# Shared-key attention scores: stacked hi/lo products against whole fp32 products on alternating row halves

## The chip, the core and the metric

The program runs on one core of a Trainium2 chip. The metric is the device time of one execution in microseconds. The kernel before took 2250.57 us, the median of 3 runs (2250.23 to 2251.85).

## The reference

Four transformer layers in fp32 over 256 tokens and a model width of 1024: two layers of a first block, then two of a second. What matters here is attention in which four query heads of 64 dimensions share one key head:

```python
# first block, per layer: 8 query heads, 2 key heads, window of 128, sinks
q = apply_rope(rms_norm(to_heads(sw_q, SWA_HEADS), q_norm_g[l]), cos, sin)
k = apply_rope(rms_norm(to_heads(sw_k, SWA_KV_HEADS), k_norm_g[l]), cos, sin)
scores = jnp.einsum('bnqkgd,bnskd->bnkgqs', qb, k_band).astype(jnp.float32) * scale
...
# second block (NSA), per layer: 8 query heads, 2 key groups, three branches
s = jnp.einsum('btghd,bngd->bghtn', qi, k_cmp).astype(jnp.float32) * scale   # compressed
s = jnp.einsum('btghd,bgtnd->bghtn', qi, k_sel).astype(jnp.float32) * scale  # selected
s = jnp.einsum('btghd,bsgd->bghts', qi, k_win).astype(jnp.float32) * scale   # window
return g_blk[..., 0:1] * o_cmp + g_blk[..., 1:2] * o_slc + g_blk[..., 2:3] * o_win
```

With 256 tokens, the selected and the window branch each come to causal attention over all keys, and the compressed branch has 15 keys, held as 16. The first block also has stick-breaking attention with 8 heads that each own their keys; the second has a gated MLP, a short convolution, latent attention (MLA, 8 heads with their own keys), and cross attention.

## The kernel before, in words

The core has three SBUF pools by size and eight PSUM banks. A bank (128 partitions x 512 fp32) is taken by `b.ps()`, in rotation. `mm` (L413) issues every matmul and `tr` (L419) every transpose. Large products are split: a value is rounded to fp32r (hi) by ACT (`split`, L570), and DVE subtracts it to get the rest (lo, L571); products of hi and lo parts are one pass each. A product of plain fp32 operands runs as two passes on TensorE, so one `mm` shows as two MATMULs in the trace.

`attend` runs four-head groups in rounds. Round r does the weights of group r-1 (scale the probabilities, L1610; transpose them; split them), the values of group r-2, the scores of group r, the preparation of group r+1, and then fills the gap with pieces of other matrix products (`gap`). The order of instructions on each engine is the order of this code. A layer of the first block has 2 groups of class `SharedHeads`, in rounds with 2 of `StickBreaking`; a layer of the second block has 4 `SharedHeads` groups and 2 of `OwnHeads` (MLA), in the order nsa, mla, nsa, nsa, mla, nsa. That is 12 `SharedHeads` groups in all. The generator `compressed` runs beside the second block's rounds.

The scores of a `SharedHeads` group, for 4 heads and two halves m of the queries:

- `stack_queries` has ACT round the transposed queries (L845) onto one half of the 128 rows and DVE put the rest (L846) on the other half, for each key head. `stack_keys` copies the first 128 keys onto both halves in fp32 (L855), the rounded keys onto both halves (L856, L857), and the rest of the keys on one half (L858).
- `SharedHeads.scores` then does, for m = 0, four fp32 products of 128 rows and 128 columns in one bank; for m = 1, in two more banks and per head, one fp32r product of 128 rows and 256 columns, and one of 64 rows with the rest of the keys.
- `softmax` reads the three banks with eight DVE operations, one for each m and head (`masked`, L816), and ACT exponentiates each.

`StickBreaking.scores` is written in another way: each of its heads lies on rows 0 to 63 or 64 to 127 by its parity, the products are plain fp32 of 64 rows, consecutive ones alternate between the two row halves, and they go to four banks. Per group these are four products of 256 columns and four of 128.

`SharedHeads.values` multiplies the weights with v: a product of 128 output rows for the hi part of the weights, and one of 64 for the lo part. `own_values`, for groups whose heads own their keys, has heads with even number use 64 output rows and odd ones 128; its last product is plain fp32.

Of the kernel before, what the change touches and what calls it, by code (L numbers as in the profile page):

```python
# [17 lines left out]
ALU = mybir.AluOpType  # L18
# [244 lines left out]
class Build:  # L263
# [546 lines left out]
    def masked(self, ps, mask, n, w, factor, first, nm):  # L810


        p = self.t("b2", [P, n, w])
        t = self.masks["window" if mask == "window" else "causal"][:, 2 * P - w:]
        for i in range(n):
            self.nc.vector.tensor_tensor_reduce(p[:, i], ps[:, i * w:i * w + w], t, factor(i), first(i), ALU.add, ALU.min,  # L816
                                                nm[:, i:i + 1])
        return p
# [18 lines left out]

    def stack_queries(self, dst, ps, m):


        nc = self.nc
        for g in range(2):
            r, o = slice(64 * g, 64 * g + 64), slice(64 - 64 * g, 128 - 64 * g)
            c = slice(m * P, m * P + P)
            nc.scalar.copy(dst[g][r, :, c], ps[r])  # L845
            nc.vector.tensor_sub(dst[g][o, :, c], ps[r], dst[g][r, :, c].bitcast(F32))  # L846

    def stack_keys(self, dst, lo, first, ps):


        nc = self.nc
        for g in range(2):
            r, o = slice(64 * g, 64 * g + 64), slice(64 - 64 * g, 128 - 64 * g)
            for x in (r, o):
                nc.scalar.copy(first[g][x], ps[r][..., :P])  # L855
            nc.scalar.copy(dst[g][r], ps[r])  # L856
            nc.scalar.copy(dst[g][o], ps[r])  # L857
            nc.vector.tensor_sub(lo[r], ps[r], dst[g][r].bitcast(F32))  # L858
# [44 lines left out]
    def block1(self, l):  # L903
# [20 lines left out]
        swk = [self.t("b1", [P, S], F32R) for _ in range(2)]  # L924
        swk_lo = self.t("b1", [P, S], F32R)
        swk_first = [self.t("h", [P, P]) for _ in range(2)]
# [5 lines left out]
        def evac_q(m, ps):  # L932
# [4 lines left out]
            qr[m] = self.t("b2", [P, 4, 2, 64])  # L937
            self.rope_pairs(qr[m], raw[m], tab[:, 0, m])

        def evac_k(m, ps):  # L940
# [13 lines left out]
            kr[m] = self.t("b1", [P, 2, 64])  # L954
            self.rope(kr[m], ko, tab[:, 1, m, 0], tab[:, 1, m, 1], 2, 64)
# [40 lines left out]
        def swa_group(q):  # L996
            r = slice(64 * q, 64 * q + 64)
            g = SharedHeads(self, 4 * q, swq[q], r, swk[q], swk_lo[r], swk_first[q],
# [42 lines left out]

    def rope_pairs(self, dst, src, tab):

        nc = self.nc
        t, u = self.t("b2", [P, 8, 64]), self.t("b2", [P, 8, 64])
        bc = lambda ap, n: ap.unsqueeze(1).broadcast_to((P, 8, n))
        cos, sin = tab[:, 0], tab[:, 1]
        nc.vector.tensor_mul(t, src, bc(cos, 64))
        nc.vector.tensor_mul(u[:, :, :32], src[:, :, 32:], bc(sin[:, :32], 32))
        nc.vector.tensor_mul(u[:, :, 32:], src[:, :, :32], bc(sin[:, 32:], 32))  # L1050
        r = lambda ap: ap.rearrange("p (b a) d -> p a b d", b=2)
        nc.vector.tensor_add(dst, r(t), r(u))
# [30 lines left out]
    def mixing(self, l):  # L1083
# [25 lines left out]
        def evac_nq(m, ps):  # L1109
            a = self.t("b2", [P, 8, 64])  # L1110
            nc.vector.tensor_add(a.rearrange("p h d -> p (h d)"), ps, bias[1])
            nq[m] = self.t("b2", [P, 4, 2, 64])
            cos, sin = self.c("rope_c", m, 64), self.c("rope_s", m, 64)
            self.rope_pairs2(nq[m], a, cos, sin)
# [6 lines left out]
        def evac_nk(m, ps):  # L1121
# [6 lines left out]
            nks[m] = self.t("b1", [P, 256])  # L1128
            self.rope(nks[m].rearrange("p (h d) -> p h d", h=4), a.rearrange("p a b d -> p (a b) d"),
                      self.c("rope_c", m, 64), self.c("rope_s", m, 64), 4, 64)  # L1130
# [23 lines left out]
        nqs = [self.t("b4", [P, 4, S], F32R) for _ in range(2)]  # L1154
        for m in range(2):
            ps = self.ps()
            for k in range(4):
                self.tr(ps[:, k * P:k * P + P], nq[m][:, k].rearrange("p b d -> p (b d)"))
            self.stack_queries(nqs, ps.rearrange("p (k t) -> p k t", k=4), m)
        nks_hi = [self.t("b2", [P, 2, S], F32R) for _ in range(2)]  # L1160
        nks_lo = self.t("b2", [P, 2, S], F32R)
        nks_first = [self.t("b1", [P, 2, P]) for _ in range(2)]
        ps = self.ps()
        for j in range(2):
            for m in range(2):
                self.tr(ps[:, (2 * j + m) * P:(2 * j + m + 1) * P], nks[m][:, j * P:j * P + P])
        self.stack_keys(nks_hi, nks_lo, nks_first, ps.rearrange("p (a t) -> p a t", a=2))
# [73 lines left out]
        def nsa_group(q, j):  # L1241
            r = slice(64 * q, 64 * q + 64)
            g = SharedHeads(self, 4 * q, nqs[q], r, nks_hi[q][:, j], nks_lo[r, j], nks_first[q][:, j],
# [38 lines left out]

    def rope_pairs2(self, dst, src, cos, sin):
        nc = self.nc
        t, u = self.t("b2", [P, 8, 64]), self.t("b2", [P, 8, 64])
        bc = lambda ap, n: ap.unsqueeze(1).broadcast_to((P, 8, n))
        nc.vector.tensor_mul(t, src, bc(cos, 64))
        nc.vector.tensor_mul(u[:, :, :32], src[:, :, 32:], bc(sin[:, :32], 32))
        nc.vector.tensor_mul(u[:, :, 32:], src[:, :, :32], bc(sin[:, 32:], 32))
        r = lambda ap: ap.rearrange("p (b a) d -> p a b d", b=2)  # L1290
        nc.vector.tensor_add(dst, r(t), r(u))
# [279 lines left out]
class FourHeads(Group):  # L1571
# [5 lines left out]
    def softmax(self, pss):  # L1577
# [7 lines left out]
        for ps, (at, n, w) in zip(pss, self.bank):  # L1585
            p = b.masked(ps, self.mask, n, w, lambda i: self.factor((at + i) // 4, (at + i) % 4), least(at),
# [26 lines left out]
class OwnHeads(FourHeads):  # L1613
# [7 lines left out]
    def scores(self):  # L1621
# [7 lines left out]
        self.softmax(pss)  # L1629
# [20 lines left out]
    def values(self):  # L1650
        b = self.b
        ops = b.ps(), b.ps()
        for h in range(4):
# [8 lines left out]
class SharedHeads(FourHeads):  # L1662
# [4 lines left out]

    def __init__(self, b, h0, q, r, k, k_lo, k_first, v, scale, mask, sinks=None, gate=None):
        self.b, self.h0, self.q, self.r, self.k, self.k_lo, self.k_first, self.v = b, h0, q, r, k, k_lo, k_first, v
# [264 lines left out]
```

## Time and profile before

| | |
|---|---|
| median of 3 runs | 2250.57 us (2250.23 to 2251.85) |
| profiled execution, own time | 2251.73 us |
| span of its trace | 2249.9 us |
| PE busy | 2209.7 us, 98% |
| weight loads (PEld) | 1868.7 us, 83% |
| DVE / ACT / POOL busy | 1532.9 (68%) / 1092.4 (49%) / 114.0 (5%) us |
| mean granted TensorE clock | 0.995 |
| DMA | 399.91 MB, mean 178 GB/s |

The profiled execution lies 1.16 us over the median of the runs. PE's busy time is a union of modelled intervals: a matmul's shown duration (390 ns for 512 columns, say) includes its way through the array, and the next one starts before it ends. What a matmul takes of PE's time is therefore read from one start to the next. A row of the timeline groups consecutive instructions of one engine, line and operation; it prints the shape of the first of them alone. PEld rows are the weight loads, PEclk is the granted clock as a share of full speed (1.00 is 2.4 GHz, 0.50 is 1.2 GHz).

### The profile page before, as it was taken

What the parts mean: (1) busy time and instruction counts of PE and PEld (TensorE: products, weight loads), DVE (VectorE), ACT (ScalarE), POOL (GpSimd) and SP (SyncE); (2) the same over time, 40 slices, a digit from 0 to 9 for tenths busy, and PEclk for the clock granted to TensorE, in tenths of its full rate; (3) what the DMA queues carried; (4) which work ended last, traced back from release to release, by engine and by line L of the source; (5) the groups of instructions that cost most, each with busy time, mean ns of one, the idle gap of its engine ahead of it and who ended that gap; (6) DMA issues with size and microseconds to landing.
All of it is one profiled execution on the core that took longest, in us unless ns stands there. A gap on an engine that the chain in (4) does not pass through costs nothing. (4 is left out here: it accounts for less than half of the span.)

```text
span 2249.9 us, 30643 instructions
## 1 busy us (share of the span) xinstructions
PE 2209.7 (98%) x11442; PEld 1868.7 (83%) x11442; DVE 1532.9 (68%) x2488; ACT 1092.4 (49%) x1713; POOL 114.0 (5%) x189
## 2 busy tenths in 40 slices
PE   7999999999999999999999999999999999999998
PEld 6878888878888888889888888888878888897886
DVE  8677457768545545987877765575478787787555
ACT  5664445583434434465654444444345665444442
POOL 2000001000000000023000000000001310000000
PEclk9999999999999999999999999999999999999999
DMA  7356465445455555644456455555545544754461
GB/s 252 130 168 193 168 225 169 138 147 181 175 198 174 195 193 201 197 147 144 158 179 215 155 183 206 206 170 192 220 159 178 164 151 137 230 189 157 178 243 47
DMA packets 114709, 399.91 MB, mean 178 GB/s; under 512 B 13056, under 2 KB 13728, under 8 KB 114560
## 3 DMA queue, kind: packets, MB, share of 16 engines
q1 hardware_dynamic: 107712, 374.30, 48.8%
q0 software_dynamic: 6848, 23.66, 3.2%
q8 instruction: 90, 1.47, 0.3%
q14 instruction: 59, 0.48, 0.1%
HBM read 396.85 MB, written 1.05 MB: 177 GB/s over the span
## 5 line engine op out<-in xcount | busy, mean ns | idle before, releaser
L413 PE MATMUL ps<-b,b 128*128 128x512 f32 (+5 forms) x10380 | 2110.2, 363 | 7.1 <-DVE b L571 2.5
L413 PEld LDWEIGHTS ps<-b,b 128*128 128x128 f32 (+1 forms) x10380 | 1749.7, 188 | 324.8 <-issue 5.9
L318 DVE TENSOR_TENSOR b<-raw,b 128x1024 fp32r<-128x1024 f32 (+3 forms) x738 | 844.3, 1181 | 53.9 <-PE ps L413 31.9
L325 ACT CAST b<-raw 128x1024 fp32r<-128x1024 f32 (+3 forms) x738 | 717.0, 1019 | 187.0 <-PE ps L413 132.6
L570 ACT CAST b<-ps 128x512 fp32r<-128x512 f32 (+2 forms) x188 | 100.6, 571 | 390.5 <-PE ps L419 319.5
L571 DVE TENSOR_TENSOR b<-ps,b 128x512 fp32r<-128x512 f32 (+2 forms) x188 | 118.6, 662 | 196.1 <-ACT b L570 195.5
L574 DVE SCALAR_TENSOR_TENSOR b<-ps,b 128x512 fp32r<-128x512 f32 (+1 forms) x64 | 39.1, 652 | 257.5 <-ACT b L573 257.5
L573 ACT ACTIVATE b<-ps 128x512 fp32r<-128x512 f32 (+1 forms) x64 | 33.1, 569 | 344.4 <-PE ps L419 344.4
L419 PE MATMUL ps<-cst,b 128*128 128x128 f32 (+1 forms) x798 | 105.5, 274 | 12.9 <-DVE b L665 11.2
L419 PEld LDWEIGHTS ps<-cst,b 128*128 128x128 f32 (+1 forms) x798 | 92.5, 140 | 24.8 <-DVE b L665 11.4
L601 POOL DMA_DIRECT2D b<-in_rows_dram x55 | 29.7, 543 | 1376.5 <-PE ps L413 932.6
L1590 ACT ACTIVATE b<-b,sm 128x128 f32<-128x128 f32 (+1 forms) x128 | 56.6, 446 | 7.2 <-DVE sm L816 7.1
L784 DVE TENSOR_TENSOR b<-b,ps 128x512 f32<-128x512 f32 (+1 forms) x48 | 30.8, 642 | 38.4 <-PE ps L413 37.2
L900 ACT ACTIVATE b<-b 128x512 f32<-128x512 f32 x32 | 20.2, 630 | 50.7 <-DVE b L898 50.7
L898 DVE TENSOR_TENSOR b<-ps,b 128x512 f32<-128x512 f32 x32 | 22.0, 689 | 27.4 <-PE ps L413 27.3
L650 DVE BATCH_NORM_STATS2 sm<-x 128x6 f32<-128x512 f32 x48 | 32.7, 689 | 4.1 <-DMA x<-in_x_dram 3.8
L773 ACT ACTIVATE b<-ps 128x512 f32<-128x512 f32 x32 | 19.3, 604 | 28.4 <-PE ps L413 28.4
L782 ACT ACTIVATE b<-ps 128x512 f32<-128x512 f32 (+1 forms) x48 | 26.9, 561 | 11.6 <-PE ps L413 11.6
L1610 DVE TENSOR_TENSOR b<-b,sm 128x512 f32<-128x512 f32 x48 | 32.0, 698 | 0.3
L783 DVE SCALAR_TENSOR_TENSOR b<-b,ps 128x512 f32<-128x512 f32 (+1 forms) x48 | 30.7, 639 | 0.0
L774 DVE SCALAR_TENSOR_TENSOR b<-ps,b 128x512 f32<-128x512 f32 x32 | 21.8, 688 | 12.6 <-ACT b L773 12.6
L419 PE MATMUL ps<-cst,x 128*128 128x128 f32 x128 | 19.6, 287 | 10.4 <-DVE x L670 10.3
(182 smaller groups left out, 786.5 us busy)
## 6 DMA issues: line engine op xcount, KB each, us to landing
raw<-in_ffn_w_dram SPq DMA_DIRECT2D x248, 512.0 KB, 5.5
raw<-in_w_in_dram SPq DMA_DIRECT2D x184, 512.0 KB, 4.5
raw<-in_w_up_dram SPq DMA_DIRECT2D x64, 512.0 KB, 5.1
raw<-in_w_down_dram SPq DMA_DIRECT2D x64, 512.0 KB, 4.9
b<-in_rows_dram POOLq DMA_DIRECT2D x19, 512.0 KB, 7.6
raw<-in_w_out_dram SPq DMA_DIRECT2D x16, 512.0 KB, 4.5
raw<-in_ffn_w_dram SPq DMA_DIRECT2D x32, 256.0 KB, 3.0
raw<-in_w_o_dram SPq DMA_DIRECT2D x16, 512.0 KB, 5.6
```

The costliest lines, as they stand in the source:

```text
L318: self.nc.vector.tensor_sub(lo[:, :n], r[:, :n], hi[:, :n].bitcast(F32))
L325: self.nc.scalar.copy(hi[:, :n], r[:, :n])
L413: i = self.nc.tensor.matmul(out, lhsT, rhs, start=start, stop=stop, skip_group_check=True)
L419: i = self.nc.tensor.transpose(out, in_, self.ident[:k, :k])
L570: nc.scalar.copy(hi, src)
L571: nc.vector.tensor_sub(lo, src, hi.bitcast(F32))
L573: nc.scalar.activation(hi, src, AF.Copy, scale=scale)
L574: nc.vector.scalar_tensor_tensor(lo, src, scale, hi.bitcast(F32), op0=ALU.mult, op1=ALU.subtract)
L650: nc.vector.bn_stats(st[:, 6 * i:6 * i + 6], x[:, c])
L784: nc.vector.tensor_mul(h[:, :w], r[:, :w], pss[1])
L1590: nc.scalar.activation(p[:, i], p[:, i], AF.Exp, scale=-1.0, bias=nm[:, at + i:at + i + 1], accum_out=den[:, at + i:at + i + 1])
L1610: e.tensor_mul(p, p, rinv[:, at:at + n].unsqueeze(2).broadcast_to((P, n, w)))
```

## The change

- `SharedHeads.scores` issues eight plain fp32 products of 64 rows: head h on row half h % 2, 128 columns for m = 0 and 256 for m = 1, into bank 2m + h % 2 of four. Consecutive products alternate between the row halves.
- Queries are no longer stacked or split: the transposed pairs of heads are copied once by ACT. `rope_pairs` and `rope_pairs2` go; `rope` takes their place.
- The keys' `rope` writes each key head twice, side by side (`twice=True`), so that a transpose brings it onto both row halves: 2 more transposes per layer of the first block, 4 more per layer of the second. One or two ACT copies then replace `stack_keys`.
- `SharedHeads.values` issues all hi products, then all lo ones. `OwnHeads.values` and `StickBreaking.values` take their heads in the order 0, 2, 1, 3.
- `compressed`: the 16 compressed keys of the two groups lie as a block diagonal (zeros by a POOL memset) in fp32; eight fp32 products of two heads each take the place of sixteen fp32r ones, one DVE addition that of four, one bank that of two.

```diff
-    def rope(self, dst, src, cos, sin, h, d, engine=None):
+    def rope(self, dst, src, cos, sin, h, d, engine=None, twice=False):
...
+        if twice:
+            t, u = (a.unsqueeze(2).broadcast_to((P, h, 2, d)) for a in (t, u))
         e.tensor_add(dst, t, u)
...
-        swq = [self.t("b4", [P, 4, S], F32R) for _ in range(2)]
+        swq = self.t("b4", [P, 4, S])
         for m in range(2):
             ps = self.ps()
             for k in range(4):
-                self.tr(ps[:, k * P:k * P + P], qr[m][:, k].rearrange("p b d -> p (b d)"))
-            self.stack_queries(swq, ps.rearrange("p (k t) -> p k t", k=4), m)
+                self.tr(ps[:, k * P:k * P + P], qr[m][:, 2 * k:2 * k + 2].rearrange("p b d -> p (b d)"))
+            nc.scalar.copy(swq[:, :, m * P:m * P + P], ps.rearrange("p (k t) -> p k t", k=4))
         ps = self.ps()
-        for m in range(2):
-            self.tr(ps[:, m * P:m * P + P], kr[m].rearrange("p b d -> p (b d)"))
-        self.stack_keys(swk, swk_lo, swk_first, ps[:, :S])
+        for q in range(2):
+            for m in range(2):
+                self.tr(ps[:, (2 * q + m) * P:(2 * q + m + 1) * P], kr[m][:, q].rearrange("p b d -> p (b d)"))
+        nc.scalar.copy(swk, ps.rearrange("p (q t) -> p q t", q=2))
...
     def values(self):
         b = self.b
         ops = b.ps(), b.ps()
-        for h in range(4):
+        for h in (0, 2, 1, 3):
...
     def scores(self):
         b, nc = self.b, self.b.nc
-        pss = [b.ps() for _ in range(3)]
-        for h in range(4):
-            o = pss[0][:, h * P:h * P + P]
-            b.mm(o, self.q[:, h, :P].bitcast(F32), self.k_first, h == 0, True)
-        for h in range(4):
-            o = pss[1 + h // 2][:, h % 2 * S:h % 2 * S + S]
-            b.mm(o, self.q[:, h, P:], self.k, h % 2 == 0, False)
-            b.mm(o, self.q[self.r, h, P:], self.k_lo, False, True)
-        self.softmax(pss)
+        r = lambda h: slice(64 * (h % 2), 64 * (h % 2) + 64)
+        q = lambda h: self.q[r(h), (self.h0 + h) // 2]
+        pss, src = [b.ps() for _ in range(4)], []
+        for m in range(2):
+            w = m * P + P
+            for h in range(4):
+                o = pss[2 * m + h % 2][:, h // 2 * w:h // 2 * w + w]
+                b.mm(o, q(h)[:, m * P:m * P + P], self.k[r(h), :w], h < 2, True)
+                src.append(o)
+        self.softmax(src)
...
         self.ops = [b.ps(), b.ps()]
-        for m in range(2):
-            pts = [(s, hi, lo) for mm, s, hi, lo in self.pt if mm == m]
-            for s, hi, lo in pts:
-                b.mm(self.ops[m], self.v(s), hi, s == 0, False)
-            for s, hi, lo in pts:
-                b.mm(self.ops[m][:64], self.v(s)[:, :64], lo, False, s == m)
+        for m, s, hi, lo in self.pt:
+            b.mm(self.ops[m], self.v(s), hi, s == 0, False)
+        for m, s, hi, lo in self.pt:
+            b.mm(self.ops[m][:64], self.v(s)[:, :64], lo, False, s == m)
...
-    for g in range(2):
-        ps = b.ps()
-        for m in range(2):
-            for h in range(4):
-                o = (m * 4 + h) * 32
-                b.mm(ps[:, o:o + 32], nqs[g][:, h, m * P:m * P + P], kt[:, g].rearrange("p a n -> p (a n)"), True, True)
...
+    ps = b.ps()
+    for m in range(2):
+        for i in range(4):
+            o = (m * 4 + i) * 32
+            b.mm(ps[:, o:o + 32], nqs[:, i, m * P:m * P + P], kt[:, i // 2].rearrange("p e n -> p (e n)"), True, True)
```

Two places in the order of instructions. The first is PE at the scores of the first `SharedHeads` group of the first layer. Before, `h_160` is the doubled first keys, `b_29_157` the rounded keys, `b_31_159` the rest of them, and `b_128_604` the stacked queries:

```order
321 L413 MATMUL ps_840<-h_160,b_128_604 128x128 x4
322 L413 MATMUL ps_841<-b_29_157,b_128_604 128x256
323 L413 MATMUL ps_841<-b_31_159,b_128_604 128x256
324 L413 MATMUL ps_841<-b_29_157,b_128_604 128x256
325 L413 MATMUL ps_841<-b_31_159,b_128_604 128x256
326 L413 MATMUL ps_842<-b_29_157,b_128_604 128x256
327 L413 MATMUL ps_842<-b_31_159,b_128_604 128x256
328 L413 MATMUL ps_842<-b_29_157,b_128_604 128x256
329 L413 MATMUL ps_842<-b_31_159,b_128_604 128x256
```

The same place after the change, where `b_29_157` is the doubled keys and `b_124_600` the queries:

```order
323 L413 MATMUL ps_822<-b_29_157,b_124_600 128x128
324 L413 MATMUL ps_823<-b_29_157,b_124_600 128x128
325 L413 MATMUL ps_822<-b_29_157,b_124_600 128x128
326 L413 MATMUL ps_823<-b_29_157,b_124_600 128x128
327 L413 MATMUL ps_824<-b_29_157,b_124_600 128x256
328 L413 MATMUL ps_825<-b_29_157,b_124_600 128x256
329 L413 MATMUL ps_824<-b_29_157,b_124_600 128x256
330 L413 MATMUL ps_825<-b_29_157,b_124_600 128x256
```

The twelve products, four of them plain fp32, have become eight that are all plain fp32; the products around them stand where they stood.

The second place is ACT ahead of the first group of the second block's first layer. Before, L845 rounds queries, and L855 to L857 make the keys of key head 0 (`b_1814_8614`) and then of key head 1 (`b_1815_8615`):

```order
657 L845 CAST b_1810_8594<-ps_8596 64x4x128
658 L845 CAST b_1810_8594<-ps_8605 64x4x128
659 L855 COPY b_1817_8617<-ps_8619 64x256 x2
660 L845 CAST b_1811_8595<-ps_8596 64x4x128
661 L856 CAST b_1814_8614<-ps_8619 64x512
662 L845 CAST b_1811_8595<-ps_8605 64x4x128
663 L857 CAST b_1814_8614<-ps_8619 64x512
664 L570 CAST b_1822_8639<-ps_8641 128x512
```

After the change, L1125 copies the queries and L1132 the keys:

```order
645 L1125 COPY b_1804_8546<-ps_8547 128x4x128
646 L1125 COPY b_1804_8546<-ps_8553 128x4x128
647 L1132 COPY b_1807_8559<-ps_8560 128x512
648 L1132 COPY b_1807_8559<-ps_8566 128x512
649 L570 CAST b_1812_8577<-ps_8579 128x512
```

Between the split that ends the stage before and the next split (L570), eight ACT instructions have become four.

## Rows read from the trace of the kernel before

**Rows 1.** The page, part 1: busy us of each engine, share of the span, instructions.
```profile
PE 2209.7 (98%) x11442; PEld 1868.7 (83%) x11442; DVE 1532.9 (68%) x2488; ACT 1092.4 (49%) x1713; POOL 114.0 (5%) x189
```

**Rows 2.** Waits of PE: line, releaser, us in total, times, longest us.
```profile
PE ps L419 <- DVE b L665: 11.2, 2, 9.6
...
PE ps L413 <- ACT b L857: 1.7, 2, 0.8
```

**Rows 3.** Timeline of PE, two shared-key rounds, first layer: start, us, group.
```profile
70.26 1.05 PE L413 MATMUL ps<-h,b 128*128 128x128 f32 x8
71.07 10.96 PE L413 MATMUL ps<-b,b 128*128 128x256 f32 x44
81.86 1.47 PE L419 MATMUL ps<-cst,b 128*128 128x128 f32 x12
83.17 1.06 PE L413 MATMUL ps<-h,b 128*128 128x128 f32 x8
```

**Rows 4.** Timeline of PE from 73.64, in the first of those rounds.
```profile
73.55 8.47 PE L413 MATMUL ps<-b,b 128*128 128x512 f32 x36
```

**Rows 5.** Timelines of PE and PEld, 97.0 to 99.6: scores of stick-breaking group.
```profile
96.79 2.37 PE L413 MATMUL ps<-b,b 128*128 128x512 f32 x19
99.09 0.61 PE L413 MATMUL ps<-r_mask_s,r_ident 128*128 128x256 bf16 x4
...
97.57 1.40 PEld L413 LDWEIGHTS ps<-b,b 64*128 64x128 f32 x16 [0.41 <-ACT b L1719]
```

**Rows 6.** Groups of PE by shape, 97.57 to 99.09: count, busy us, mean ns.
```profile
L413 PE MATMUL ps<-b,b 64*128 64x256 f32 x8 | 1.3, 402 | 0.0
L413 PE MATMUL ps<-b,b 64*128 64x128 f32 x8 | 0.8, 271 | 0.0
```

**Rows 7.** Groups of PE by shape, 114.6 to 115.5: passes on one row half.
```profile
L413 PE MATMUL ps<-b,b 64*128 64x256 f32 x4 | 1.1, 402 | 0.0
```

**Rows 8.** Timelines around the second block's first groups, both layers.
```profile
970.13 1.06 ACT L845 CAST b<-ps 64x512 fp32r<-64x512 f32 x2 [9.38 <-PE ps L419]
...
973.68 0.58 ACT L857 CAST b<-ps 64x512 fp32r<-64x512 f32 x1
...
974.31 4.16 PE L413 MATMUL ps<-b,b 128*128 128x256 f32 x17 [0.84 <-ACT b L857]
...
1730.66 1.53 PE L413 MATMUL ps<-b,b 128*128 128x256 f32 x9 [0.84 <-ACT b L857]
```

**Rows 9.** Five windows at lowered clock: us, busy of each engine, clock, DMA.
```profile
977.07:980.49 3.41, 3.41 (x11) 3.35 (x11) 3.33 (x18) 3.37 (x14) 0.00 (x0) 0.50 0.02 5
1106.78:1110.19 3.41, 3.41 (x10) 2.64 (x9) 1.19 (x2) 1.37 (x2) 0.00 (x0) 0.50 0.42 115
...
1861.13:1864.54 3.41, 3.41 (x12) 2.83 (x12) 2.26 (x5) 2.00 (x6) 0.00 (x0) 0.50 0.00 0
...
sum 17.07, PE 16.54 PEld 13.96 DVE 13.06 ACT 11.48 POOL 0.00; mean PE 3.31 PEld 2.79 DVE 2.61 ACT 2.30 POOL 0.00
```

**Rows 10.** Windows of rounds: us, busy PE, PEld, DVE, ACT, POOL, clock.
```profile
70.26:81.86 11.60, 11.60 (x53) 9.08 (x52) 9.05 (x26) 7.31 (x22) 0.00 (x0) 1.00 0.39 131
...
1077.00:1101.00 24.00, 23.96 (x133) 20.22 (x132) 21.30 (x46) 17.01 (x38) 1.65 (x3) 1.00 0.50 158
```

**Rows 11.** Timeline of PE, 1103.0 to 1106.8: compressed products.
```profile
1103.90 1.96 PE L413 MATMUL ps<-h,b 128*128 128x32 f32 x16
```

**Rows 12.** Values: groups of PE by shape, 1020.25 to 1021.7; two windows.
```profile
L413 PE MATMUL ps<-b,b 128*64 128x512 f32 x3 | 1.0, 396 | 0.0
...
1020.24:1021.73 1.49, 1.49 (x10) 1.05 (x8) 0.66 (x2) 1.49 (x4) 0.00 (x0) 1.00 0.40 162
1043.68:1046.74 3.06, 3.06 (x23) 2.34 (x22) 2.25 (x4) 1.54 (x3) 0.00 (x0) 1.00 0.97 331
```

**Rows 13.** Timeline of DVE, 69.5 to 76: it reads the first group's scores.
```profile
71.35 0.41 DVE L816 CUSTOM_DVE_ANT_0 b<-ps,r_window,sm 128x128 f32<-128x128 f32 x1 [0.94 <-PE ps L413]
...
74.59 1.22 DVE L318 TENSOR_TENSOR b<-raw,b 128x1024 fp32r<-128x1024 f32 x1
```

More of the change, by code (lines that the diff above doesn't have):

```diff
@@ L808, in attend, with masked @@
                 self.gap(gap[min(r, len(gap) - 1)])
-    def masked(self, ps, mask, n, w, factor, first, nm):
+    def masked(self, src, mask, w, factor, first, nm):
+        n = len(src)
         p = self.t("b2", [P, n, w])
@@ L815, in masked @@
         for i in range(n):
-            self.nc.vector.tensor_tensor_reduce(p[:, i], ps[:, i * w:i * w + w], t, factor(i), first(i), ALU.add, ALU.min,
+            self.nc.vector.tensor_tensor_reduce(p[:, i], src[i], t, factor(i), first(i), ALU.add, ALU.min,
                                                 nm[:, i:i + 1])
@@ L923, in block1 @@
         sw_v = self.t("b2", [P, 2, 2, 2, 64], F32R)
-        swk = [self.t("b1", [P, S], F32R) for _ in range(2)]
-        swk_lo = self.t("b1", [P, S], F32R)
-        swk_first = [self.t("h", [P, P]) for _ in range(2)]
+        swk = self.t("b2", [P, 2, S])
         raw = {}
@@ L936, in evac_q @@
             nc.scalar.copy(raw[m].rearrange("p h d -> p (h d)"), ps)
-            qr[m] = self.t("b2", [P, 4, 2, 64])
-            self.rope_pairs(qr[m], raw[m], tab[:, 0, m])
+            qr[m] = self.t("b2", [P, 8, 64])
+            self.rope(qr[m], raw[m], tab[:, 0, m, 0], tab[:, 0, m, 1], 8, 64)
         def evac_k(m, ps):
@@ L953, in evac_k @@
             nc.vector.tensor_mul(ko, ko, r[:, 8:10].unsqueeze(2).broadcast_to((P, 2, 64)))
-            kr[m] = self.t("b1", [P, 2, 64])
-            self.rope(kr[m], ko, tab[:, 1, m, 0], tab[:, 1, m, 1], 2, 64)
+            kr[m] = self.t("b1", [P, 2, 2, 64])
+            self.rope(kr[m], ko, tab[:, 1, m, 0], tab[:, 1, m, 1], 2, 64, twice=True)
         self.gemm_first(xt, [("w_in", 0, evac_q), ("w_in", 1, evac_k)], l)
@@ L1127, in evac_nk @@
             self.split(nv[m][:, :, 0], nv[m][:, :, 1], f)
-            nks[m] = self.t("b1", [P, 256])
-            self.rope(nks[m].rearrange("p (h d) -> p h d", h=4), a.rearrange("p a b d -> p (a b) d"),
-                      self.c("rope_c", m, 64), self.c("rope_s", m, 64), 4, 64)
+            nks[m] = self.t("b2", [P, 4, 2, 64])
+            self.rope(nks[m], a.rearrange("p a b d -> p (a b) d"),
+                      self.c("rope_c", m, 64), self.c("rope_s", m, 64), 4, 64, twice=True)
         def evac_nc(m, ps):
@@ L1151, in mixing @@
         self.gap(9000)
-        nqs = [self.t("b4", [P, 4, S], F32R) for _ in range(2)]
+        nqs = self.t("b4", [P, 4, S])
         for m in range(2):
@@ L1157, in mixing @@
             for k in range(4):
[L1158 to L1163, printed above, removed]
-        for j in range(2):
-            for m in range(2):
-                self.tr(ps[:, (2 * j + m) * P:(2 * j + m + 1) * P], nks[m][:, j * P:j * P + P])
-        self.stack_keys(nks_hi, nks_lo, nks_first, ps.rearrange("p (a t) -> p a t", a=2))
+                self.tr(ps[:, k * P:k * P + P], nq[m][:, 2 * k:2 * k + 2].rearrange("p b d -> p (b d)"))
+            nc.scalar.copy(nqs[:, :, m * P:m * P + P], ps.rearrange("p (k t) -> p k t", k=4))
+        nkt = self.t("b4", [P, 4, S])
+        for j in range(2):
+            ps = self.ps()
+            for q in range(2):
+                for m in range(2):
+                    self.tr(ps[:, (2 * q + m) * P:(2 * q + m + 1) * P], nks[m][:, 2 * j + q].rearrange("p b d -> p (b d)"))
+            nc.scalar.copy(nkt[:, 2 * j:2 * j + 2], ps.rearrange("p (q t) -> p q t", q=2))
         kp = self.ps()
@@ L1575, with softmax @@
     sinks = gate = None
-    def softmax(self, pss):
+    def softmax(self, src):
         b, nc = self.b, self.b.nc
@@ L1584, in softmax @@
         self.p = []
-        for ps, (at, n, w) in zip(pss, self.bank):
-            p = b.masked(ps, self.mask, n, w, lambda i: self.factor((at + i) // 4, (at + i) % 4), least(at),
+        for at, n, w in self.bank:
+            p = b.masked(src[at:at + n], self.mask, w, lambda i: self.factor((at + i) // 4, (at + i) % 4), least(at),
                          nm[:, at:at + n])
@@ L1628, in scores @@
             b.mm(pss[1 + h // 2][:, h % 2 * S:h % 2 * S + S], q[:, h, P:], k[:, h], h % 2 == 0, True)
-        self.softmax(pss)
+        self.softmax([pss[0][:, h * P:h * P + P] for h in range(4)]
+                     + [pss[1 + h // 2][:, h % 2 * S:h % 2 * S + S] for h in range(4)])
     def weights(self):
@@ L1790, in values @@
         ops = b.ps(), b.ps()
-        for k in range(4):
+        for k in (0, 2, 1, 3):
             i, e = k // 2, k % 2
@@ L1807, in compressed @@
     ws, xs = [], []
+    kt = b.t("h", [P, 2, 2, 16])
+    nc.gpsimd.memset(kt, 0.0)
     for j in range(2):
```

64 lines of the change are left out of this document (11 added, 53 removed).

## The prediction, written before the changed kernel was run

> **What bounds the kernel now.** I read the busy times first, then the list of PE's waits, then PE's timeline around the places that the change touches. PE is busy for 2209.7 of 2249.9 us [rows 1], and the other engines have slack on average. PE's longest waits, 11.2 us in two places for DVE's L665, lie where the change touches nothing; of the waits it touches, only that for ACT's L857 shows, 1.7 us in two places [rows 2]. So time is gained here by what PE itself no longer does, and lost where PE would have to wait.
>
> In a shared-key round the reader is to see that the scores are dearer than their columns. They start at 70.26; the eight passes of the four fp32 products of 128 columns end at 71.07 [rows 3], 0.10 us each. The group after them has 44 products, and the later look from 73.64 counts 36 that start at 73.55 [rows 3, 4]: the eight fp32r products of 256 columns thus took 73.55 - 71.07 = 2.48 us, 0.31 each. The 36 products of 512 columns that follow take (81.86 - 73.55) / 36 = 0.231 each, so one of 256 should take 0.116. The 0.19 more that each takes falls where 128 rows and 64 rows alternate. The whole of the scores is 73.55 - 70.26 = **3.29 us per group**.
>
> **What the new scores cost.** The new form is not in these groups, but the stick-breaking groups of the same kernel issue just that: eight passes of 256 and eight of 128 columns on 64 rows [rows 6], alternating between the halves and into four banks, as 16 weight loads show [rows 5]. From 96.79 to the next step at 99.09 there are 19 products, 16 of them these passes [rows 5]: 2.30 - 3 x 0.231 = **1.61 us**, the change to 64 rows and back included. The saving is 3.29 - 1.61 = 1.68 per group, and with 12 groups 20.2 us. I take that row since shapes, alternation and banks agree.
>
> The ends: where four passes of 256 columns stand on one row half alone they take 1.1 us [rows 7], 0.27 each; if the halves did not overlap, 8 x 0.27 + 8 x 0.14 = 3.3 us, and the saving is nothing. If they overlap and the changes of rows cost nothing, four pairs of 0.27 and four of 0.10 are 1.5 us, a saving of 1.8 per group, 21.5 in all.
>
> **Transposes.** Doubled keys need 2 more per layer of the first block and 4 more per layer of the second: 12. Twelve take 83.17 - 81.86 = 1.31 us [rows 3], and they stand on PE's path: +1.3.
>
> **The first group of the second block.** PE waited 0.84 us in each layer for L857, the last of eight ACT instructions that began at 970.13; L857 began at 973.68, and PE would have started at 974.31 - 0.84 = 973.47 [rows 8]. Now four copies are due; with 0.58 each they are done by some 970.13 + 4 x 0.6 = 972.5. The wait goes: -1.7. Next in line is PE's own work, 1 us later.
>
> **Edits that I cost at nothing.** ACT's and DVE's stacking goes (L845, L846, L855 to L858), and DVE writes the keys' rope twice as wide; both lie beside PE, with DVE at 68% and ACT at 49% [rows 1]. If that cover failed, the wait would show at L1132's copies; it is bounded by today's 0.84 per layer. SP's queue is unchanged; POOL gets one memset per layer and is 5% busy [rows 1].
>
> The compressed products: sixteen passes of 32 columns took 1.96 us with the last one's way through the array [rows 11], some (1.96 - 0.27) / 15 = 0.11 each, as long as a transpose of 128 columns. Eight fp32 products are again sixteen passes: 0. The freed bank and the three fewer DVE additions relieve no wait that shows.
>
> The order of the values cuts the changes between 128 and 64 output columns from 4 to 2 per group. For shared groups, six products of 512 columns, three of them with 64 output columns, took 1.49 us [rows 12] against 6 x 0.231 = 1.39, with the step from the transposes in it: at most 0.10 for four changes, and 12 x 0.05 = 0.6 us to gain. For groups with own keys, 20 passes took 3.06 us [rows 12] against 12 x 0.116 + 8 x 0.10 = 2.2, so 0.86 more. In the new order each 64-column head still goes from its fp32r products to its fp32 one and back. I take 0 by the shared groups' row, where the change of columns stands alone; the other end is half of 0.86 for 8 groups, 3.4, in all -4.0.
>
> By the Trainium skill, "TensorEngine Tiling (Array Packing)", section Tiling Modes, changing the tiling mode drains the engine, and 128 x 64 is another mode than 128 x 128. By that rule every change of columns would cost as a change of rows does, and the new order would gain; the row of the shared groups, 0.10 us for four changes, does not bear it out.
>
> The clock: five stretches of 3.41 us each ran at 0.50, that is at 1.2 GHz, 17.07 us in all [rows 9]. Each costs half its length, 1.7 us. Three of them (977.07, 1106.78, 1861.13) follow a group's scores: the first the 0.84 us wait and the scores behind it [rows 8], the second, and by the same place the third, the scores and compressed products that end near 1105.7 [rows 11]. With other products there they may go or come elsewhere. I take 0; the ends are -5.1 (three go) and +3.4 (two more come).
>
> **The sum.** 2251.73 (the profiled execution) - 20.2 + 1.3 - 1.7 = 2231.1 us. The profiled execution lies 1.16 over the median, so the median goes to **2230.0 us**, 0.9% under 2250.57. With the scores' price between 1.5 and 1.8 us and one stretch of low clock more or fewer, this case alone gives 2226 to 2234.
>
> **Rivals.**
>
> *DVE becomes the bound of the rounds.* In the first round DVE is busy for 9.05 of 11.60 us, in the tightest for 21.30 of 24.00 [rows 10]. Take 1.68 off PE: 9.05 of 9.92, and 21.30 of 22.3 with one group in it. What speaks for it: 95% there, and the chain from scores through DVE, ACT and DVE to the transposes doesn't shrink. Against: 0.9 us is still spare in the first round, and PE hardly waits for DVE in the rounds now. If half the scores' gain is given back: 2230.0 + 10.1 = 2240.
>
> *The clock stretches behind the scores go.* 2230.0 - 5.1 = 2225. For: two of the three follow products with many changes of rows; against: nothing shows that it is those, and two of the five stretches lie elsewhere.
>
> *Changes of output columns cost.* If each costs 0.86 / 4 = 0.21 us in shared groups too, 2 fewer changes in 12 + 8 groups give 8.4 us: 2222. For: the own-key groups' 0.86; against: the shared groups' 0.10 [rows 12]. That is the rule of the Trainium skill's page named above.
>
> *The halves do not overlap here.* The queries and keys lie otherwise in SBUF than the stick-breaking ones. The scores then cost about 3.3 us as before: 2230.0 + 20.2 = 2250, no change. Against: only the addresses differ from the row that I took.
>
> *Slower: four banks held.* One more of the eight banks is taken from a group's scores until DVE has read it. DVE began on the first group at 71.35 and was done at 74.59 [rows 13], 3.2 us. If the rotation then hands PE a bank that DVE still holds, PE waits in each group; it decides from 1.7 us per group, and at the full 3.2 the time is 2230.0 + 12 x 3.2 = 2268. For: eight banks in fixed rotation, and preparation products that need one each. Against: the stick-breaking groups hold four banks today, and PE waits for none of DVE's L816 in the list.
>
> **How the numbers follow.** The forecast case has 0.67; DVE as the bound 0.12; the clock 0.09; changes of columns 0.05; no overlap 0.03; four banks 0.04. This kernel's measurement can tell about 0.2%, 4.5 us, from no change: faster means under 2246.1. The first four cases are faster, 0.92 with a little of DVE's case taken off; no overlap and the weak forms of the bank case make 0.04 the same; slower 0.04. The range from 2221.5 to 2238 holds the forecast case with its bounds, the clock and column cases, and the part of DVE's case that gives back up to 8 us; outside lie the rest of it, no overlap and four banks, less than 0.2.
>
> **What would show it.** In the changed profile: a group's scores as 16 passes of 64 rows in about 1.6 us; PE's busy time down by about 19; no wait for L1132 in the list; compressed products still at 1.8 us from start to next start; the number of windows at 0.50. Wrong, if the passes of one pair start a full pass apart (no overlap), if PE waits for DVE's L571, L816 or L1564 in the rounds (DVE, or the banks), or if the values take visibly less than 1.49 and 3.06 us (columns).

## The result, and the profile after

The changed kernel took **2228.53 us** (median of 4 runs, 2225.89 to 2228.81) against 2251.21 for the kernel before (4 runs beside it): a ratio of 0.9893 with a 95% interval from 0.9878 to 0.9907 (taken over the runs; the two medians alone give 0.9899). The forecast was 2230.0, 2221.5 to 2238.0. The profiled execution took 2228.81 us, 22.9 under that of before; its span is 2227.0.

Busy times of the changed kernel (the page, part 1), against [rows 1]:

```profile
PE 2187.6 (98%) x11454; PEld 1852.9 (83%) x11454; DVE 1520.3 (68%) x2456; ACT 1078.1 (48%) x1681; POOL 118.7 (5%) x191
```

PE lost 22.1 us of busy time, DVE 12.6, and PE is busy for 98% as before: the gain was PE's own work.

Weight loads (PEld) of the changed kernel over the first two shared-key rounds, where a load stands for each pass:

```profile
71.15 1.18 PEld L413 LDWEIGHTS ps<-b,b 64*128 64x128 f32 x16 [0.35 <-issue]
72.66 8.03 PEld L413 LDWEIGHTS ps<-b,b 128*128 128x128 f32 x36 [0.33 <-issue]
80.73 1.46 PEld L419 LDWEIGHTS ps<-cst,b 128*128 128x128 f32 x12
82.36 1.33 PEld L413 LDWEIGHTS ps<-b,b 64*128 64x128 f32 x16 [0.17 <-issue]
84.02 1.00 PEld L413 LDWEIGHTS ps<-b,b 128*128 128x128 f32 x5 [0.33 <-issue]
```

The 16 passes of the first group last 72.66 - 71.15 = 1.51 us to the next product of 128 rows; with the change to 64 rows ahead of them (the product before starts 0.32 ahead in place of 0.23) that is the 1.6 us that the stick-breaking groups gave. The second group takes 84.02 - 82.36 = 1.66.

The same rounds in PE's timeline, against [rows 3]:

```profile
80.96 1.47 PE L419 MATMUL ps<-cst,b 128*128 128x128 f32 x12
82.36 10.12 PE L413 MATMUL ps<-b,b 64*128 64x128 f32 x52
92.32 0.82 PE L419 MATMUL ps<-cst,b 128*128 128x128 f32 x6
93.30 0.85 PE L419 MATMUL ps<-cst,b 128*128 128x128 f32 x6 [0.17 <-DVE b L1564]
```

From the scores to the transposes the first round takes 80.96 - 71.15 = 9.81 us in place of 11.60. The second ends with a short wait for DVE's L1564, which is L1610 of the kernel before.

PE's waits, against [rows 2] (L667 and L672 are the L665 and L670 of before, DVE's L629 is the rope that writes the keys twice):

```profile
PE ps L419 <- DVE b L667: 11.6, 2, 9.9
PE ps L419 <- DVE x L672: 10.4, 9, 2.5
...
PE ps L419 <- DVE b L629: 0.5, 1, 0.5
PE ps L419 <- DVE b L1564: 0.3, 2, 0.2
PE ps L413 <- PE ps L413: 0.3, 2, 0.2
```

Two rows of the same list of the kernel before, where the rope stands at L627 and the scaling of the weights at L1610:

```profile
PE ps L419 <- DVE b L1610: 0.4, 2, 0.3
PE ps L419 <- DVE b L627: 0.3, 1, 0.3
```

The wait for L857 is gone. Only PE's wait for its own scores (0.3 us in two places) is new; that for the rope grew from 0.3 to 0.5 us. ACT's copies ahead of the second block's first group, and the group's first loads, against [rows 8]:

```profile
965.25 1.07 ACT L1125 COPY b<-ps 128x512 f32<-128x512 f32 x2 [8.90 <-PE ps L419]
...
966.21 1.10 ACT L1132 COPY b<-ps 128x512 f32<-128x512 f32 x2
...
968.00 1.18 PEld L413 LDWEIGHTS ps<-b,b 64*128 64x128 f32 x16 [0.36 <-issue]
```

The copies end at 967.3, PE comes at 968.0.

The windows at lowered clock, against [rows 9]:

```profile
1280.87:1284.28 3.41, 3.41 (x11) 2.50 (x9) 3.37 (x7) 3.25 (x5) 0.00 (x0) 0.50 0.00 0
1673.40:1676.81 3.41, 3.41 (x11) 2.91 (x10) 2.00 (x7) 0.64 (x2) 0.00 (x0) 0.50 0.55 185
2028.38:2031.80 3.41, 3.41 (x13) 2.71 (x13) 3.02 (x7) 2.34 (x4) 0.00 (x0) 0.50 0.00 0
sum 10.24, PE 10.24 PEld 8.13 DVE 8.39 ACT 6.22 POOL 0.00; mean PE 3.41 PEld 2.71 DVE 2.80 ACT 2.07 POOL 0.00
```

Five stretches have become three. The three behind shared-key scores are gone; one has come at 1673, in a feed-forward stage that the change does not touch. (The last 4 to 8 us of each trace, in which PE has no more work, show 0.50 as well; they cost nothing and are not counted.)

Where the 22.9 us went, from the starts of the same products in both traces: the twelve groups' scores -19.5, with 3.29 taken for each before; what the second block's first groups gained beyond that, their wait included, -0.6 per layer; transposes and the wait for L629 +1.6; the clock -3.4, half of 17.07 - 10.24. That is -22.5; the remaining 0.4 lies in steps of under 0.5 us of both signs.

### The profile page after: what moved, and what is told of

It is laid out like the page before. It is cut to its first block, busy times and chain, and to the rows that moved or that the text cites. A ratio compares the mean times of both kernels' runs of the same rounds, so it can differ in the third digit from the quotient of the medians.

```text
span 2227.0 us, 30615 instructions
## 1 busy us (share of the span) xinstructions
PE 2187.6 (98%) x11454; PEld 1852.9 (83%) x11454; DVE 1520.3 (68%) x2456; ACT 1078.1 (48%) x1681; POOL 118.7 (5%) x191
## 5 line engine op out<-in xcount | busy, mean ns | idle before, releaser
L413 PE MATMUL ps<-b,b 128*128 128x512 f32 (+7 forms) x10412 | 2090.1, 363 | 5.4 <-DVE b L571 2.5
L413 PEld LDWEIGHTS ps<-b,b 128*128 128x128 f32 (+2 forms) x10412 | 1736.8, 188 | 316.3 <-issue 11.3
L570 ACT CAST b<-ps 128x512 fp32r<-128x512 f32 (+2 forms) x188 | 100.8, 571 | 394.6 <-PE ps L419 313.7
L571 DVE TENSOR_TENSOR b<-ps,b 128x512 fp32r<-128x512 f32 (+2 forms) x188 | 118.7, 663 | 194.8 <-ACT b L570 194.4
L879 DVE TENSOR_TENSOR b<-ps,b 128x512 f32<-128x512 f32 x32 | 22.1, 689 | 27.1 <-PE ps L413 27.0
L1564 DVE TENSOR_TENSOR b<-b,sm 128x512 f32<-128x512 f32 x48 | 34.2, 740 | 0.3
L776 DVE SCALAR_TENSOR_TENSOR b<-ps,b 128x512 f32<-128x512 f32 x32 | 21.8, 688 | 12.6 <-ACT b L775 12.6
L419 PE MATMUL ps<-cst,x 128*128 128x128 f32 x128 | 19.5, 286 | 10.5 <-DVE x L672 10.4
```

The lines of the kernel that those rows point to most:

```text
L413: i = self.nc.tensor.matmul(out, lhsT, rhs, start=start, stop=stop, skip_group_check=True)
L419: i = self.nc.tensor.transpose(out, in_, self.ident[:k, :k])
L570: nc.scalar.copy(hi, src)
L571: nc.vector.tensor_sub(lo, src, hi.bitcast(F32))
L1564: e.tensor_mul(p, p, rinv[:, at:at + n].unsqueeze(2).broadcast_to((P, n, w)))
```

## The experiments

Times are compared as ratios to the kernel before that ran beside each variant; the changed kernel's is 0.9893. An interval reaches about 0.0015 to either side, 3.4 us.

**Two products on one row half, then two on the other.** Does the gain need the alternation?

```diff
-            for h in range(4):
+            for h in (0, 2, 1, 3):
                 o = pss[2 * m + h % 2][:, h // 2 * w:h // 2 * w + w]
                 b.mm(o, q(h)[:, m * P:m * P + P], self.k[r(h), :w], h < 2, True)
```

> The changed kernel with the same eight score products per group, in the same four banks, but in the order of heads 0, 2, 1, 3 for each half of the queries: two products (four passes) on one row half, then two on the other. Theory (the gain is that the two row halves work at once): only neighbouring passes across a change of half overlap, so a group's 16 passes need about 7 x 0.109 + 7 x 0.21 = 2.2 us in place of the 1.3 us that four pairs of each width need in the trace after; about 0.9 us more per group, 11 us in 12 groups, some 2239 us. In the timeline the scores last about 2.4 us from start to next start in place of 1.51. Rival (the gain is only the changes of rows that are no longer made, and alternation does nothing): within 2 us of the changed kernel's 2228.5.

Measured: 2229.35 us, ratio 0.9892 (0.9877 to 0.9907). The weight loads of the first group:

```profile
71.37 1.28 PEld L413 LDWEIGHTS ps<-b,b 64*128 64x128 f32 x16 [0.35 <-issue]
72.98 0.30 PEld L413 LDWEIGHTS ps<-b,b 128*128 128x128 f32 x2 [0.33 <-issue]
```

72.98 - 71.37 = 1.61 us, 0.10 more than with alternation, not 0.9. The theory as I put it falls: strict alternation isn't needed. The rival isn't shown by it either, since the passes of 128 columns still start in pairs 13 ns apart, while program order has four passes of one half first. So I asked next what one half alone costs, and how far the order can be bent.

**All on one half.**

```diff
-        r = lambda h: slice(64 * (h % 2), 64 * (h % 2) + 64)
+        r = lambda h: slice(0, 64)
```

> The changed kernel with all eight score products of a group on row half 0; the odd heads take the queries of the even ones, so their scores are not the reference's. Nothing else moves. Theory (the two halves run at once, and a half's own passes stand one behind the other at 0.216 us for 256 columns and 0.109 for 128, as single products of the stick-breaking groups show): the 16 passes need 8 x 0.216 + 8 x 0.109 = 2.6 us in place of 1.3, so 1.3 more per group, 15.6 in all, about 2244 us. Rival (passes cost the same on one half or two, and only the changes between 128 and 64 rows were saved, some 1.1 us per group by the run that grouped them): no change from 2228.5 us.

Measured: 2241.56 us, ratio 0.9948 (0.9933 to 0.9963). Loads of the first group, and PE's groups by shape from 71.42 to 74.22:

```profile
71.42 2.48 PEld L413 LDWEIGHTS ps<-b,b 64*128 64x128 f32 x16 [0.35 <-issue]
74.23 0.30 PEld L413 LDWEIGHTS ps<-b,b 128*128 128x128 f32 x2 [0.33 <-ACT b L1544]
```

```profile
L413 PE MATMUL ps<-b,b 64*128 64x256 f32 x8 | 1.9, 376 | 0.0
L413 PE MATMUL ps<-b,b 64*128 64x128 f32 x8 | 1.2, 285 | 0.0
```

The scores take 74.23 - 71.42 = 2.81 us, 1.30 more than after, as worked out; passes start 0.112 and 0.216 apart, each behind the other. Twelve times 1.30 is 15.6. The time rose by 0.0055 of 2251, 12.4 us, and the intervals allow 15.6. Between the two profiled executions the rise is 2239.28 - 2228.81 = 10.5 us; there this kernel has no stretch at lowered clock while PE works and the changed one has three, worth 5.1 us, so that the rise without them is 15.6. That the halves work at once is settled, and with it that the alternation's purpose is met as long as both halves have work at hand.

**The halves as blocks.**

```diff
+        out = {}
+        for e in range(2):
+            for m in range(2):
+                w = m * P + P
+                for h in (e, e + 2):
+                    o = out[m, h] = pss[2 * m + e][:, h // 2 * w:h // 2 * w + w]
+                    b.mm(o, q(h)[:, m * P:m * P + P], self.k[r(h), :w], h < 2, True)
```

> The changed kernel with all four products of row half 0 ahead of all four of row half 1 in program order (the run with two and two showed no loss). Theory now (TensorE takes up the work of the idle half although the other half's passes stand ahead of it in program order): with eight passes ahead in place of four, either still no loss, 2228.5 us, or, if it looks ahead by about four passes only, half of the overlap is lost: some 0.5 to 0.7 us per group, 6 to 8 us, 2235 to 2237 us. Rival (no look-ahead at all; the run before overlapped for another reason): the scores of one half follow the other, 2.6 us per group, 15 us slower.

Measured: 2232.83 us, ratio 0.9908 (0.9893 to 0.9923).

```profile
71.68 1.73 PEld L413 LDWEIGHTS ps<-b,b 64*128 64x128 f32 x16 [0.35 <-issue]
73.74 0.30 PEld L413 LDWEIGHTS ps<-b,b 128*128 128x128 f32 x2 [0.33 <-ACT b L325]
```

2.06 us, in this group as in the other eleven: 0.55 more than the first group after, 0.75 less than one half alone. In the trace the first four passes of half 0 start 0.11 to 0.21 apart with nothing beside them; half 1, whose first pass is the ninth in program order, begins 6 ns behind the fifth, ahead of three passes of half 0. By the scores' length the middle case of what was expected holds. The time rose less than its 6 to 8 us, by 0.0015, 3.4 us, which alone can't be told from no change; the trace decides here.

**The 64-row rests behind the 128-row products, in the kernel before.**

```diff
             b.mm(o, self.q[:, h, P:], self.k, h % 2 == 0, False)
+        for h in range(4):
+            o = pss[1 + h // 2][:, h % 2 * S:h % 2 * S + S]
             b.mm(o, self.q[self.r, h, P:], self.k_lo, False, True)
```

> The kernel before with one thing moved: for the second half of the queries the four fp32r products of 128 rows come first, then the four of 64 rows with the rest of the keys; operands, banks and all else as before. Theory (each change between 128 and 64 rows costs about 0.19 us): changes per group fall from eight to two, 6 x 0.19 x 12 = 13.7 us, some 2237 us, and the scores last some 2.1 to 2.2 us per group. Rival (the 64-row fp32r products are slow in themselves): 2251 us, as before. On the side: PE's wait for L857 ahead of the second block's first group stays; if the stretch at lowered clock behind it goes with the changes of rows, it was not the wait that brought it.

Measured: 2242.11 us, ratio 0.9949 (0.9932 to 0.9965), 11.5 us under the kernel before with an interval from 7.9 to 15.3. PE's timeline of the first round, from two windows; then PE's waits:

```profile
70.68 1.05 PE L413 MATMUL ps<-h,b 128*128 128x128 f32 x8
...
72.80 8.48 PE L413 MATMUL ps<-b,b 128*128 128x512 f32 x36
```

```profile
PE ps L419 <- DVE b L1610: 4.4, 6, 1.1
...
PE ps L413 <- ACT b L857: 1.7, 2, 0.8
```

The scores last 72.80 - 70.68 = 2.12 us, so 1.17 of the 1.68 us per group comes from changing between 128 and 64 rows twice in place of eight times. That the rest of the keys adds onto what the product before it wrote is not the reason: in the kernel before, the steps from such a product to the next head's, which shares no output with it, take 0.31 us as well. Times 12 the gain is 14.0, within the interval; PE now waits 4.4 us for DVE's scaling of the weights, where before that was 0.4, which is enough to explain why less arrives. These waits stand in the second block (1.06 us at 994.25, 0.99 at 1038.93, and the same places a layer on). The changed kernel, with still shorter scores, waits 0.3. Here DVE still does the stacking, and the last products of a group finish all banks late; which of the two it is was not tried. On the side: the wait for L857 stands as before, but the window from 972 to 982 has the clock at 1.00:

```profile
972.00:982.00 10.00, 10.00 (x78) 9.73 (x77) 9.63 (x29) 9.68 (x29) 1.26 (x2) 1.00 0.06 13
```

So, as far as one execution tells, that wait alone does not bring the stretch at 977.

**The orders of the values undone.**

```diff
-        for h in (0, 2, 1, 3):
+        for h in range(4):
...
-        for m, s, hi, lo in self.pt:
-            b.mm(self.ops[m], self.v(s), hi, s == 0, False)
-        for m, s, hi, lo in self.pt:
-            b.mm(self.ops[m][:64], self.v(s)[:, :64], lo, False, s == m)
+        for m in range(2):
+            pts = [(s, hi, lo) for mm, s, hi, lo in self.pt if mm == m]
+            for s, hi, lo in pts:
+                b.mm(self.ops[m], self.v(s), hi, s == 0, False)
+            for s, hi, lo in pts:
+                b.mm(self.ops[m][:64], self.v(s)[:, :64], lo, False, s == m)
```

> The changed kernel with the orders of the values as before: lo products behind each half of the queries in the shared-key groups, heads 0, 1, 2, 3 in the groups with own keys. Theory (these orders are worth nothing, as the aligned traces show no step there): 2228.5 us within 2 us. Rival (a change between 64 and 128 output columns costs about 0.2 us): 5 to 8 us slower, 2233 to 2237. A smaller gain of the new order in the groups with own keys alone would show as up to 3.4 us.

Measured: 2227.18 us, ratio 0.9885 (0.9870 to 0.9899). The orders are worth nothing that can be measured: the intervals exclude the 5 to 8 us of the rival.

**More work for DVE.**

```diff
         self.softmax(src)
+        t = b.t("b2", [P, 4, P])
+        for _ in range(2):
+            nc.vector.tensor_mul(t, self.p[0], self.p[0])
```

> The changed kernel with two more DVE operations of 128 x 512 (0.69 us each) behind the eight that read a group's scores; their results are not used. Rival of the forecast (DVE is already the bound of the rounds): 12 x 1.4 = 17 us slower, about 2245 us. Theory (DVE still has room in most rounds, but little in the second round of the first block, where PE waits 0.33 us ahead of the transposes in the trace after): only those rounds and the tightest of the second block give way, 3 to 8 us slower, 2231 to 2236 us.

Measured: 2229.86 us, ratio 0.9895 (0.9880 to 0.9910). DVE's list shows the added work, and PE's waits do not:

```profile
L1642 DVE TENSOR_TENSOR b<-b 128x512 f32<-128x512 f32 x24 | 16.5, 688 | 0.1
```

```profile
PE ps L419 <- DVE b L1564: 0.4, 2, 0.2
```

16.5 us more on DVE cost PE 0.1 us of waiting for L1564. Both what was expected and the rival fail: not even the tight rounds gave way. DVE's share of a round says little about its being late.

**Six banks.**

```diff
-        pss, src = [b.ps() for _ in range(4)], []
+        pss, src = [b.ps() for _ in range(6)], []
...
-                o = pss[2 * m + h % 2][:, h // 2 * w:h // 2 * w + w]
-                b.mm(o, q(h)[:, m * P:m * P + P], self.k[r(h), :w], h < 2, True)
+                o = pss[h % 2][:, h // 2 * w:h // 2 * w + w] if m == 0 else pss[2 + h][:, :w]
+                b.mm(o, q(h)[:, m * P:m * P + P], self.k[r(h), :w], m == 1 or h < 2, True)
```

> The changed kernel with six PSUM banks for a group's scores in place of four (each product of 256 columns has a bank of its own). Theory (banks are no limit here): within 2 us of the changed kernel's 2228.5, with no new wait of PE. Rival (the eight banks are close to used up by four): PE waits for DVE's eight operations on the scores or for the splits, 1 to 3 us per group, 2240 to 2265 us.

Measured: 2234.44 us, ratio 0.9915 (0.9900 to 0.9930), 5 us over the changed kernel. Loads of the first block's second group:

```profile
82.05 0.89 PEld L413 LDWEIGHTS ps<-b,b 64*128 64x128 f32 x12 [0.17 <-issue]
83.24 0.29 PEld L413 LDWEIGHTS ps<-b,b 64*128 64x128 f32 x2 [0.30 <-DVE b L571]
83.84 0.29 PEld L413 LDWEIGHTS ps<-b,b 64*128 64x128 f32 x2 [0.30 <-DVE b L571]
84.47 0.53 PEld L413 LDWEIGHTS ps<-b,b 128*128 128x128 f32 x3 [0.33 <-issue]
```

The group takes 84.47 - 82.05 = 2.42 us in place of 1.66: its last products wait for banks that the split of the weights (L571) still reads. So the place and the releaser of the bank rival are real, at six banks, and the theory that banks are no limit falls; eight of the twelve groups take 1.92 to 2.67 us in the trace, 5.6 us more in all, less than the rival's range. With four the limit is just touched: the same group's 1.66 in place of 1.51.

**Keys doubled by copies, a try at a faster version.** The keys are transposed once and copied onto both halves; the orders of the values are those of before. Of the diff, the second block's part:

```diff
-        for j in range(2):
-            ps = self.ps()
-            for q in range(2):
-                for m in range(2):
-                    self.tr(ps[:, (2 * q + m) * P:(2 * q + m + 1) * P], nks[m][:, 2 * j + q].rearrange("p b d -> p (b d)"))
-            nc.scalar.copy(nkt[:, 2 * j:2 * j + 2], ps.rearrange("p (q t) -> p q t", q=2))
+        ps = self.ps()
+        for j in range(2):
+            for m in range(2):
+                self.tr(ps[:, (2 * j + m) * P:(2 * j + m + 1) * P], nks[m][:, 2 * j:2 * j + 2].rearrange("p b d -> p (b d)"))
+        k4 = nkt.rearrange("p (j q) t -> p j q t", j=2)
+        for q in range(2):
+            for e in range(2):
+                d, x = k4[64 * e:64 * e + 64, :, q], ps[64 * q:64 * q + 64].rearrange("p (j t) -> p j t", j=2)
+                nc.vector.tensor_copy(d, x)
```

> A try at a faster version: the changed kernel with the keys transposed once, as before, and copied from PSUM onto both row halves (by ACT in the first block, by DVE in the second), so that the 12 added transposes go; and with the orders of the values as before the change, which cost nothing when undone. Expected from the aligned traces: -1.3 for the transposes, -0.5 for PE's wait for the rope (L629), nothing for the orders: 2226.7 us if nothing else waits. Rival (the copies end too late for the first group of the second block): up to 0.8 us per layer given back, no gain that can be measured.

Measured: 2227.69 us, ratio 0.9887 (0.9871 to 0.9904), which can't be told from the changed kernel. The transposes are gone, and a wait has come:

```profile
PE ps L419 <- DVE b L1569: 1.6, 3, 0.7
```

L1569 is the scaling of the weights (L1564 of the changed kernel, 0.3 us there): 1.3 us more of waiting for DVE, which now does the second block's copies, against 1.3 us of transposes saved and 0.2 less of waiting for the rope. Whether the copies are what delays it was not tried.

**Both kernels again, for the clock.**

> The kernel before, unchanged, profiled once more: where do the stretches at lowered clock lie? Theory (they come and go from execution to execution, since the runs so far had between none and five of them, at other places each, and none when the scores were slowest): fewer or more than five, and not all at the five places of the first trace. Rival (they belong to the products of this kernel, so that the change itself took two of them away): five again, near 977, 1107, 1295, 1861 and 2052 us.

> The changed kernel, unchanged, profiled once more. Theory (the stretches come and go): not the same three as in the first trace. Rival (they belong to the kernel): three again, near 1281, 1673 and 2028 us.

Measured: 2251.39 and 2226.89 us. The windows at lowered clock of the kernel before, and of the changed one:

```profile
977.01:980.42 3.41, 3.41 (x10) 2.96 (x11) 3.15 (x18) 3.35 (x14) 0.00 (x0) 0.50 0.00 0
1106.71:1110.13 3.42, 3.42 (x10) 2.63 (x9) 1.61 (x3) 1.05 (x3) 0.00 (x0) 0.50 0.30 78
1686.98:1690.39 3.41, 3.41 (x9) 2.94 (x10) 1.94 (x6) 1.17 (x2) 0.00 (x0) 0.50 0.77 241
2052.20:2055.62 3.42, 3.42 (x9) 2.64 (x9) 3.42 (x7) 2.92 (x4) 0.00 (x0) 0.50 0.00 0
```

```profile
1279.49:1282.90 3.41, 3.41 (x12) 2.85 (x13) 2.94 (x6) 2.18 (x4) 0.00 (x0) 0.50 0.00 0
2027.01:2030.42 3.41, 3.41 (x10) 2.57 (x9) 3.36 (x7) 3.15 (x5) 0.00 (x0) 0.50 0.00 0
```

Neither theory holds whole. In the kernel before, the stretches at 977, 1107 and 2052 came back, those at 1295 and 1861 did not, and one at 1687 was new; product for product it lies within 1 us of the one at 1673 in the changed kernel. In the changed one two of three came back. So in two traces of a kernel some places had a stretch twice, others once. The two places behind scores in the second block's first layer (977 and 1107) had one in both traces of the kernel before and in neither of the changed one. Again the changed kernel has two fewer, 3.4 us. The other traces bear that out: while PE works, the kernel before has 5 and 4 stretches and its variant with the grouped rests 4, the changed kernel 3 and 2 and its seven variants 0 to 3. The mean granted clock of single executions was 0.994 to 0.997 for the kernel before and 0.997 or 0.998 for the changed one, with the seven variants between 0.995 and 0.999.

## Why the prediction was right, point by point

- **The scores.** 1.61 us per group was read from another class of the same kernel, and 1.6 came; -20.2 was worked out, -19.5 measured, and this one term carries the result. What falls short are the second groups of the first block (1.66 for 1.51, a bank just late) and 0.2 us ahead of the compressed products, where PE waits for its own scores (the last row of the waits above).
- **What the saving consists of** was right, and the runs give the parts: of 3.29 us, grouping the rests takes 1.17 off (2.12). Whole fp32 products on one half would take 2.81, and the second half working at once takes 1.30 off that (1.51).
- **The end "halves do not overlap"** was mis-sized: I took 0.27 us per pass of 256 columns from four passes in 1.1 us, which includes the changes of rows at both ends; behind each other they start 0.216 apart. By the scores' length that rival would have been about 5 us faster than before, not equal to it; the run on one half was 0.0052, 11.7 us, under the kernel before, and its profile has none of the five stretches at lowered clock that cost that kernel 8.5 us.
- **Transposes** 1.3 as worked out; the rope of the keys, now twice as wide, was among the edits that I costed at nothing, and PE's wait for it grew by 0.2 us.
- **The first group of the second block**: the wait went, with the copies done 0.7 us ahead, but 1.2 us arrived in place of 1.7. I had taken 3.29 us for these two groups as for the others. In the trace of before, eight passes of 128 rows stand in a row behind the wait, 0.12 us apart from 974.31 on, and the passes change rows six times, not eight: at 0.19 us a change these scores were some 0.4 us cheaper and had less to give.
- **The clock**: I took 0 with -5.1 as an end; two stretches fewer, -3.4, came, in two pairs of traces. This is the term that was off. Between the profiled executions 20.6 us were forecast and 22.9 came: 3.4 more for the clock and 0.4 of small steps, against 0.7 less for the scores, 0.5 less for the first groups and 0.3 more for transposes and rope. The median lies only 1.5 us under the forecast because the profiled execution was 1.16 us over the median before and 0.28 after. That these misses partly cancel is luck; none of them is near the size of the scores' term. In the profiles of the other variants, none lay behind the second block's first scores; behind the compressed products the grouped rests had one in each layer and the six banks one in all. What brings them was not settled: not the length of the scores, since the run on one half had none there, and, by one execution, not the wait for L857 alone.
- **The orders of the values**: 0 was right: undoing them gave 0.9885 against 0.9893, and the 20 passes of the own-key group of [rows 12] took 3.09 us in the changed kernel against 3.06. Most of the 0.86 us that I saw there and could not place lies at the plain fp32 products of 64 output columns: in the changed kernel the step into one takes 0.21 us where 0.12 is usual, and the step out 0.20 where 0.11 is. Between fp32r products, steps from 64 to 128 columns and back keep their pace (0.24 and 0.23 us in the shared groups of before, against 0.231). Either order has as many of those fp32 products, so there was little to gain. The Trainium skill ("TensorEngine Tiling (Array Packing)", Tiling Modes) says that changing the tiling mode drains the engine. For rows (128 against 64) the runs agree, 0.2 us a change; for the columns of fp32r products they show no such cost.
- **DVE as the bound** is refuted for this kernel: 16.5 us more on DVE changed nothing that can be measured (0.9895 against 0.9893); with stacking still on DVE and the rests grouped, PE did wait 4.4 us for it. My argument from its busy share of 95% in a window was weak.
- **The bank rival** named the right resource; it decides at six banks, not at four.

## What to carry to other kernels

Price a new form of an operation by a place in the same kernel that already issues it, with the changes into it and out of it in the price. Count how often TensorE changes between 128-row and 64-row products, since each change cost 0.2 us here, and give both row halves work within a few passes of each other. For a rival in which another engine becomes the bound, look at when its result is needed rather than at its busy share.

## What the runs showed that I had not expected

- TensorE took up work for the idle row half ahead of program order: with four passes of the other half ahead nothing was lost but 0.1 us, and with eight ahead, half 1 began beside the fifth pass, ahead of three that stand before it (2.06 us per group against 1.51 and 2.81).
- The changed kernel's first passes of a pair start 6 to 8 ns apart; in the first block's second groups a delay of 51 ns at the first 256-column product of half 1, whose weight load waits for DVE, put the halves out of step, and the 16 passes took 0.15 us longer.
